# A Mamba-2 scan beside its projections: a product moved from GpSimd to VectorE, and a norm one step later

## The chip, the cores and the metric

The kernel runs on one core of a Trainium2 chip. Its engines work at the same time, each through its own list of instructions in order: TensorE (PE; its weight loads are PEld) multiplies matrices, VectorE (DVE), ScalarE (ACT) and GpSimd (POOL) work element by element, and SyncE (SP) mostly issues DMAs. The metric is the device time of one execution in microseconds (us). Of the kernel before there are three timed runs; one further execution was profiled.

## What is computed

One layer of a hybrid decoder trunk over 1024 tokens of width 1024, in float32: a Mamba-2 (SSD) mixer, a hierarchical mixture of 64 experts, a gated per-layer embedding, and a final norm. The change touches the mixer. Cut to what matters:

```python
def ssd_mixer(u, ...):
    zxbcdt = u @ w_in                       # z, x, B, C, dt
    xbc = silu(causal_depthwise_conv(xbc, conv_w, conv_b))
    y = ssd_chunked_scan(xs, dt, A, Bm, Cm)
    yz = (y + xs * d_skip) * silu(z)
    yg = yz.reshape(L, 4 groups, 512)
    yg = yg * rsqrt(mean(yg * yg, axis=-1) + EPS)   # a norm in each group
    return (yg * gnorm) @ w_out

def ssd_chunked_scan(x, dt, A, Bm, Cm):     # chunks of 128 tokens
    acum = cumsum(dt * A)                   # within a chunk
    decay = exp(where(causal, acum_l - acum_s, -inf))
    w_ls = (C_l . B_s) * decay              # causal B-C product times decay
    y_diag = w_ls @ (x * dt)
    states = B^T @ (x * dt * decay_to_end)
    h = h * chunk_decay + states            # from chunk to chunk
    y_off = (C @ h) * exp(acum)             # reaches the output from earlier chunks
    return y_diag + y_off
```

## The kernel before

The mixer works in eight units: two halves of 512 tokens, in each four groups of eight heads. For a unit, project computes ten tiles of 128 channels (B, C, four of x, four of z), each by 24 matmuls: weights and inputs are split into a high and a low float32r part, and three products (lines 183, 184, 185) are added up over eight steps of depth. split (lines 69 and 70) makes the parts: ScalarE the high half (wh), then VectorE the low one (wl), and the third matmul of a tile (L185) is the first that needs wl. The six tiles of B, C and x then go through a convolution, three multiply-adds on VectorE (L263) and a SiLU.

While a unit is projected, the scan of the unit before it runs beside it, chunk by chunk. The function front(c) prepares a chunk: the cumulative sums come by DMA, spread over all partitions (ac); TensorE transposes x (px, L306) and B and multiplies B with C (pb, L308 and L309) into two buffers of one PSUM pool (tp, two buffers in all); ScalarE takes ec = exp(ac) (L311); VectorE subtracts each token's own sum, eight times 128x128 (L313); ScalarE takes the exponential again (L315). VectorE makes xc = x dt (L317), the masked product cbm (L321), xd (L327) and the weights ac times cbm (L330). GpSimd copies the last column of ec (ed, L325) and multiplies ec with C (L329), except for a sequence's first chunk. back(c) does the matmuls of y (L347, L349) and of the state (L352), the state's update on VectorE (L343, L354), the skip and gate (L360, L362) and the squares (ScalarE, then GpSimd's sums L366 and L367). norm adds the squares over channels on TensorE (L372) and takes the root in thirteen small VectorE instructions (lines 56 to 66); store transposes the roots (L380), scales the four chunks (L383) and writes them to DRAM by SP.

The program is written as a plan of unit steps: after each of the ten projected tiles (steps 0 to 9) the pieces listed for that step are emitted. Fronts stand at steps 0, 1, 3 and 5, backs at 2, 4, 6 and 8, norm at 9, and store at step 0 of the next unit. A scheduler then orders each engine's instructions from this, by its own reckoning of when each is ready; so the order on an engine is not the order written. The last scan runs beside the output product (lines 482 to 484) by a plan of its own.

Of the kernel before, what the change touches and what calls it, by code (L numbers as in the profile page):

```python
# [7 lines left out]
F32 = mybir.dt.float32  # L8
# [4 lines left out]
AF = mybir.ActivationFunctionType  # L13
# [5 lines left out]
DI, NH, HD, NG, NS, Q = 2048, 32, 64, 4, 128, 128  # L19
NCH = T // Q  # L20
# [21 lines left out]
class K:  # L42
# [64 lines left out]
    def ssd(self, left, right):  # L107
        nc, tc, a = self.nc, self.tc, self.a
# [18 lines left out]
        wk = self.pool("wk", 2, **kr)  # L127
# [140 lines left out]
        def project(hf, g):  # L268
            x = X[hf]
            w = load(2 * DI + g * 128, 2 * DI + 512 + g * 128)  # L270
            xT, zT = [], zp.tile([128, 4, HT], F32, name="z")
            bT = conv_tile(hf, w, 0, x, 16 + g)
            yield
            cT = conv_tile(hf, w, 1, x, 20 + g)
            U[hf, g] = bT, cT, xT, zT
            yield
            for j in range(2):
                w = load(DI + g * 512 + j * 256)
                for i in range(2):
                    xT.append(conv_tile(hf, w, i, x, 4 * g + 2 * j + i))  # L280
                    yield
            for j in range(2):
                w = load(g * 512 + j * 256)
                for i in range(2):
                    nc.scalar.activation(zT[:, 2 * j + i], proj(w, i, x), AF.Silu)
                    yield

        def scan(hf, g):

            hs = slice(8 * g, 8 * g + 8)  # L290
# [4 lines left out]
            def front(c):  # L295
                dt_s, acs = SZ[hf]
                bT, cT, xT, zT = U[hf, g]
                cg = hf * HC + c
                cs = slice(c * Q, (c + 1) * Q)
                ac = wk.tile([128, 8, Q], F32, name="ac", bufs=3)  # L300
                nc.sync.dma_start(ac, bass.AP(tensor=acd.tensor, offset=acd[8 * g:8 * g + 1, cg * Q:cg * Q + 1].offset,
                                              ap=[[0, 128], [T, 8], [1, Q]]))
                px = self.ps_tp.tile([128, 8, HD], F32, name="tp")
                pxf = px.rearrange("p h d -> p (h d)")
                for j in range(4):
                    nc.tensor.transpose(pxf[:, j * 128:(j + 1) * 128], xT[j][:, cs], self.ident)  # L306
                pb = self.ps_tp.tile([128, 2, 128], F32, name="tp")
                nc.tensor.transpose(pb[:, 0], bT[:, cs], self.ident)  # L308
                nc.tensor.matmul(pb[:, 1], lhsT=bT[:, cs], rhs=cT[:, cs], start=True, stop=True)  # L309
                ec = wk.tile([128, 8, Q], F32, name="ec")  # L310
                nc.scalar.activation(ec, ac, AF.Exp)  # L311
                for h in range(8):
                    nc.vector.tensor_scalar(ac[:, h], ac[:, h], acs[:, c, 8 * g + h:8 * g + h + 1], 0.0,  # L313
                                            op0=OP.subtract, op1=OP.min)
                nc.scalar.activation(ac, ac, AF.Exp)  # L315
                xc = wk.tile([128, 8, HD], F32, name="xc")
                nc.vector.tensor_mul(xc, px, dt_s[:, c, hs][:, :, None].to_broadcast([128, 8, HD]))  # L317
                bt = wk.tile([128, 128], F32, name="bt")
                nc.scalar.activation(bt, pb[:, 0], AF.Copy)
                cbm = wk.tile([128, 128], F32, name="cbm")  # L320
                nc.vector.tensor_mul(cbm, pb[:, 1], self.tri)  # L321
                ed = wk.tile([128, 8], F32, name="ed")
                xd = None
                if cg < NCH - 1:
                    nc.gpsimd.tensor_copy(ed, ec[:, :, Q - 1])  # L325
                    xd = wk.tile([128, 8, HD], F32, name="xd")
                    nc.vector.tensor_mul(xd, xc, ac[:, :, Q - 1:Q].to_broadcast([128, 8, HD]))  # L327
                if cg:
                    nc.gpsimd.tensor_mul(ec, ec, cT[:, cs][:, None, :].to_broadcast([128, 8, Q]))  # L329
                nc.vector.tensor_mul(ac, ac, cbm[:, None, :].to_broadcast([128, 8, Q]))  # L330
                V[c] = ac, ec, xc, bt, ed, xd

# [44 lines left out]
            def store():  # L377
# [3 lines left out]
                for c in range(HC):  # L381
# [4 lines left out]
                        yzs[c])  # L386

            return front, back, norm, store

        X, SZ, U = {}, {}, {}  # L390
# [4 lines left out]
        prev, before = None, None  # L395
        units = [(hf, g) for hf in range(2) for g in range(NG)]
        for hf, g in units:
            plan = {}

            def at(t, f, *args):  # L400
                plan.setdefault(t, []).append((f, args))

            if g == 0:
                for t in (0, 1, 7, 8):
                    at(t, next, sizes, None)
            if before:
                at(0, before[3])
            if prev:
                front, back, norm, store = prev
                for t, f, c in ((0, front, 0), (1, front, 1), (2, back, 0), (3, front, 2), (4, back, 1),  # L410
                                (5, front, 3), (6, back, 2), (8, back, 3)):
                    at(t, f, c)
                if (hf, g) != units[-1]:
                    at(9, norm)
            if hf == 0 and g == NG - 1:
                xg = x_half(1)
                for t in (4, 5, 6, 7):
                    at(t, next, xg)
            for t, _ in enumerate(project(hf, g)):
                for f, args in plan.get(t, ()):  # L420
                    f(*args)
            before, prev = prev, scan(hf, g)
            if hf == 0 and g == NG - 1:
                for _ in xg:
                    pass
                sizes = step_sizes(1)
        front, back, norm, store = prev
# [1008 lines left out]
```

## Time and profile before

| | |
|---|---|
| median of three runs | 2008.52 us (2005.11 to 2008.72) |
| profiled execution, device time | 2003.53 us |
| its span, first to last instruction | 2001.7 us |
| busy share of the span | PE 94%, DVE 53%, ACT 37%, POOL 14% |
| granted TensorE clock, mean | 0.971 |

The shares are means over stages with different limits. The stages show in the busy time of stretches: the columns are the stretch, its length, the busy us (and instructions) of PE, PEld, DVE, ACT and POOL, the granted clock, the mean share of the DMA engines and GB/s.

```profile
0.00:84.00 84.00, 68.53 (x319) 55.30 (x320) 46.32 (x90) 39.73 (x57) 17.74 (x39) 0.98 0.46 141
...
690.00:760.00 70.00, 61.68 (x331) 47.77 (x330) 56.55 (x103) 30.63 (x43) 12.77 (x14) 0.95 0.64 205
760.00:940.00 180.00, 165.27 (x835) 134.14 (x835) 120.58 (x333) 62.15 (x90) 32.03 (x54) 0.93 0.74 264
940.00:2001.00 1061.00, 1030.48 (x4329) 399.95 (x4325) 358.41 (x710) 237.19 (x396) 48.74 (x44) 0.99 0.94 376
```

Until 84 us the input is normed and the first group is projected without a scan; from there to 690 us projections and scans run side by side; then the last scan beside the output product, the rest of that product with the router, and from some 940 us the experts. In the rows of waits shown further on, the instruction in front waited for the one behind the arrow, with the sum in us, the number of waits and the longest.

### The profile page before, as it was taken

What the parts mean: (1) busy time and instruction counts of PE and PEld (TensorE: products, weight loads), DVE (VectorE), ACT (ScalarE), POOL (GpSimd) and SP (SyncE); (2) the same over time, 40 slices, a digit from 0 to 9 for tenths busy, and PEclk for the clock granted to TensorE, in tenths of its full rate; (3) what the DMA queues carried; (4) which work ended last, traced back from release to release, by engine and by line L of the source; (5) the groups of instructions that cost most, each with busy time, mean ns of one, the idle gap of its engine ahead of it and who ended that gap; (6) DMA issues with size and microseconds to landing.
All of it is one profiled execution on the core that took longest, in us unless ns stands there. A gap on an engine that the chain in (4) does not pass through costs nothing.

```text
span 2001.7 us, 23417 instructions
## 1 busy us (share of the span) xinstructions
PE 1875.6 (94%) x8822; PEld 1071.1 (54%) x8822; DVE 1060.1 (53%) x2148; ACT 740.7 (37%) x1036; POOL 273.1 (14%) x338
## 2 busy tenths in 40 slices
PE   7989987899999899997999999999999999999996
PEld 5867766677777677884343343333433334334334
DVE  5487886679889687657332341524414234233223
ACT  4466655457667543332121121211212222122123
POOL 1122223223232222011000000000000000000004
PEclk9989998899999999997999999999999999999998
DMA  5333432434543469684999999999999999998883
GB/s 173 104 91 93 118 104 63 110 95 114 130 97 89 128 197 345 225 311 163 388 421 421 373 421 400 398 419 375 420 405 395 420 383 410 415 372 323 341 324 114
DMA packets 190056, 534.73 MB, mean 267 GB/s; under 512 B 15855, under 2 KB 128497, under 8 KB 141809
## 3 DMA queue, kind: packets, MB, share of 16 engines
q1 hardware_dynamic: 175632, 510.53, 69.8%
q10 hardware_dynamic: 11008, 12.94, 1.9%
q0 software_dynamic: 3296, 9.70, 1.3%
q8 instruction: 71, 1.16, 0.2%
q14 instruction: 49, 0.39, 0.1%
HBM read 517.27 MB, written 17.69 MB: 267 GB/s over the span
## 4 chain that ended last, share of the span: by engine, by line
PE 71%; DVE 13%; DMA 7%; issue 4%; ACT 2%; POOL 2%; SPq 0%; ACTq 0%; POOLq 0%; DVEq 0%
PE pup L1004 12%; PE pgate L1004 11%; PE py L1004 11%; PE pq L885 6%; DMA ac<-acd 4%; PE mm L185 3%; PE pc L994 3%; PE mm L184 3%; PE mm L183 3%; DVE ac L313 3%; DVE xbc L263 3%; PE mm L483 3%; PE mm L484 3%; PE mm L482 2%; PE pc L838 2%
## 5 line engine op out<-in xcount | busy, mean ns | idle before, releaser
L183 PE MATMUL mm<-xh,wh 128*128 128x512 f32 x640 | 270.5, 423 | 6.0 <-ACT xh L69 5.9
L185 PE MATMUL mm<-xh,wl 128*128 128x512 f32 x640 | 257.4, 402 | 10.8 <-DVE wl L70 10.6
L184 PE MATMUL mm<-xl,wh 128*128 128x512 f32 x640 | 255.6, 399 | 1.5 <-DVE xl L70 1.5
L1004 PE MATMUL pup<-w,XT 128*64 128x512 f32 x1016 | 239.5, 598 | 0.6 <-DMA w<-in_w_up_dram 0.6
L1004 PE MATMUL pgate<-w,XT 128*64 128x512 f32 x1000 | 231.9, 599 | 0.0
L1004 PE MATMUL py<-w,hT 128*64 128x512 f32 (+1 forms) x1024 | 226.9, 585 | 2.1 <-DMA w<-in_w_down_dram 2.1
L70 DVE TENSOR_TENSOR yx<-py,yx 128x512 fp32r<-128x512 f32 (+1 forms) x68 | 44.8, 659 | 234.3 <-ACT yx L69 234.3
L1004 PEld LDWEIGHTS py<-w,hT 128*64 128x64 f32 x1024 | 70.1, 137 | 145.9 <-issue 138.3
L1004 PEld LDWEIGHTS pup<-w,XT 128*64 128x64 f32 x1016 | 72.0, 136 | 141.5 <-issue 131.7
L185 PEld LDWEIGHTS mm<-xh,wl 128*128 128x128 f32 x640 | 123.1, 192 | 43.5 <-DVE wl L70 16.8
L183 PEld LDWEIGHTS mm<-xh,wh 128*128 128x128 f32 x640 | 124.6, 195 | 37.6 <-ACT xh L69 6.1
L184 PEld LDWEIGHTS mm<-xl,wh 128*128 128x128 f32 x640 | 124.1, 194 | 33.3 <-issue 6.0
L1004 PEld LDWEIGHTS pgate<-w,XT 128*64 128x64 f32 x1000 | 68.6, 136 | 134.2 <-issue 129.6
L313 DVE TENSOR_SCALAR ac<-ac,acs 128x128 f32<-128x128 f32 x256 | 105.6, 472 | 42.0 <-ACT ec L311 42.0
L263 DVE SCALAR_TENSOR_TENSOR xbc<-raw,convw,xbc 128x512 f32<-128x512 f32 x144 | 120.6, 838 | 10.8 <-ACT xbc L261 9.9
L885 PE MATMUL pq<-wpg,vx 128*128 128x512 f32 x256 | 123.1, 607 | 0.0
L70 DVE TENSOR_TENSOR wl<-w,wh 128x1024 fp32r<-128x1024 f32 x80 | 98.0, 1227 | 41.4 <-ACT wh L69 41.3
L69 ACT ACTIVATE wh<-w 128x1024 fp32r<-128x1024 f32 x80 | 83.9, 1052 | 66.4 <-PE mm L184 63.9
L483 PE MATMUL mm<-wl,yh 128*128 128x512 f32 x256 | 101.8, 402 | 3.2 <-DVE wl L494 3.2
L482 PE MATMUL mm<-wh,yh 128*128 128x512 f32 x256 | 99.4, 407 | 3.9 <-ACT wh L493 3.9
L484 PE MATMUL mm<-wh,yl 128*128 128x512 f32 x256 | 100.8, 398 | 0.0
L69 ACT ACTIVATE yx<-py 128x512 fp32r<-128x512 f32 (+1 forms) x68 | 38.9, 572 | 159.4 <-PE py L1004 159.4
(381 smaller groups left out, 2855.1 us busy)
## 6 DMA issues: line engine op xcount, KB each, us to landing
w<-in_w_up_dram SPq DMA_DIRECT2D x127, 1024.0 KB, 9.3
w<-in_w_gate_dram SPq DMA_DIRECT2D x125, 1024.0 KB, 8.7
w<-in_w_down_dram SPq DMA_DIRECT2D x120, 1024.0 KB, 9.3
w<-in_w_in_dram SPq DMA_DIRECT2D x32, 1024.0 KB, 5.4
w<-in_w_out_dram SPq DMA_DIRECT2D x48, 512.0 KB, 4.6
ac<-acd SPq DMA_DIRECT2D x32, 512.0 KB, 9.5
w<-in_w_in_dram SPq DMA_DIRECT2D x16, 512.0 KB, 5.1
yn<-yz SPq DMA_DIRECT2D x32, 256.0 KB, 4.3
```

The costliest lines, as they stand in the source:

```text
L69: self.nc.scalar.activation(dst_h, src, AF.Copy)
L70: self.nc.vector.tensor_sub(dst_l, src, r_(dst_h))
L183: nc.tensor.matmul(ps, lhsT=wh[:, k], rhs=x[0][:, k], start=(k == 0), stop=False)
L184: nc.tensor.matmul(ps, lhsT=wh[:, k], rhs=x[1][:, k], start=False, stop=False)
L185: nc.tensor.matmul(ps, lhsT=wl[:, k], rhs=x[0][:, k], start=False, stop=(k == KD - 1))
L263: nc.vector.scalar_tensor_tensor(o, raw[:, j:j + HT], convw[:, m, j:j + 1], o, op0=OP.mult, op1=OP.add)
L313: nc.vector.tensor_scalar(ac[:, h], ac[:, h], acs[:, c, 8 * g + h:8 * g + h + 1], 0.0, op0=OP.subtract, op1=OP.min)
L482: nc.tensor.matmul(po[i][hf], lhsT=yh[:, ts], rhs=wh[:, cs], start=(k == 0), stop=False)
L483: nc.tensor.matmul(po[i][hf], lhsT=yh[:, ts], rhs=wl[:, cs], start=False, stop=False)
L484: nc.tensor.matmul(po[i][hf], lhsT=yl[:, ts], rhs=wh[:, cs], start=False, stop=(k == 15))
L885: nc.tensor.matmul(V["pq"], lhsT=V["vT"][:, k], rhs=wpg[:, k, cs], start=(k == 0), stop=(k == KD - 1))
L1004: nc.tensor.matmul(ps[64 * b:64 * b + 64], lhsT=xt(k0 + k, b), rhs=w[b][:, k, cs], start=(k0 + k == 0), stop=(k0 + k == K - 1))
```

## The change

Three edits in the scan. The product of ec and C, and the copy of ec's last column, run on VectorE in place of GpSimd. xc, bt and the masked product cbm are written ahead of the exponential and the subtractions. norm moves from step 9 to step 0 of the next unit, and store from step 0 to step 2.

```diff
@@ -307,26 +307,27 @@
                 pb = self.ps_tp.tile([128, 2, 128], F32, name="tp")
                 nc.tensor.transpose(pb[:, 0], bT[:, cs], self.ident)
                 nc.tensor.matmul(pb[:, 1], lhsT=bT[:, cs], rhs=cT[:, cs], start=True, stop=True)
+                xc = wk.tile([128, 8, HD], F32, name="xc")
+                nc.vector.tensor_mul(xc, px, dt_s[:, c, hs][:, :, None].to_broadcast([128, 8, HD]))
+                bt = wk.tile([128, 128], F32, name="bt")
+                nc.scalar.activation(bt, pb[:, 0], AF.Copy)
+                cbm = wk.tile([128, 128], F32, name="cbm")
+                nc.vector.tensor_mul(cbm, pb[:, 1], self.tri)
                 ec = wk.tile([128, 8, Q], F32, name="ec")
                 nc.scalar.activation(ec, ac, AF.Exp)
                 for h in range(8):
                     nc.vector.tensor_scalar(ac[:, h], ac[:, h], acs[:, c, 8 * g + h:8 * g + h + 1], 0.0,
                                             op0=OP.subtract, op1=OP.min)
                 nc.scalar.activation(ac, ac, AF.Exp)
-                xc = wk.tile([128, 8, HD], F32, name="xc")
-                nc.vector.tensor_mul(xc, px, dt_s[:, c, hs][:, :, None].to_broadcast([128, 8, HD]))
-                bt = wk.tile([128, 128], F32, name="bt")
-                nc.scalar.activation(bt, pb[:, 0], AF.Copy)
-                cbm = wk.tile([128, 128], F32, name="cbm")
-                nc.vector.tensor_mul(cbm, pb[:, 1], self.tri)
                 ed = wk.tile([128, 8], F32, name="ed")
                 xd = None
                 if cg < NCH - 1:
-                    nc.gpsimd.tensor_copy(ed, ec[:, :, Q - 1])
+                    nc.vector.tensor_copy(ed, ec[:, :, Q - 1])
+                if cg:
+                    nc.vector.tensor_mul(ec, ec, cT[:, cs][:, None, :].to_broadcast([128, 8, Q]))
+                if cg < NCH - 1:
                     xd = wk.tile([128, 8, HD], F32, name="xd")
                     nc.vector.tensor_mul(xd, xc, ac[:, :, Q - 1:Q].to_broadcast([128, 8, HD]))
-                if cg:
-                    nc.gpsimd.tensor_mul(ec, ec, cT[:, cs][:, None, :].to_broadcast([128, 8, Q]))
                 nc.vector.tensor_mul(ac, ac, cbm[:, None, :].to_broadcast([128, 8, Q]))
                 V[c] = ac, ec, xc, bt, ed, xd
 
@@ -404,14 +405,13 @@
                 for t in (0, 1, 7, 8):
                     at(t, next, sizes, None)
             if before:
-                at(0, before[3])
+                at(0, before[2])
+                at(2, before[3])
             if prev:
                 front, back, norm, store = prev
                 for t, f, c in ((0, front, 0), (1, front, 1), (2, back, 0), (3, front, 2), (4, back, 1),
                                 (5, front, 3), (6, back, 2), (8, back, 3)):
                     at(t, f, c)
-                if (hf, g) != units[-1]:
-                    at(9, norm)
             if hf == 0 and g == NG - 1:
                 xg = x_half(1)
                 for t in (4, 5, 6, 7):
```

What the scheduler makes of it shows in the order of instructions on an engine; out<-in are the names of the kernel, with buffer numbers. In the changed kernel the lines are numbered anew: L311 is xc, L315 cbm, L319 the subtractions, L325 the copy ed, L327 the product ec, L330 xd, L331 ac times cbm.

First place: VectorE where the first two fronts begin (ac_746 and xc_767 or xc_756 are the first front's, ac_817 the second's). Before:

```order
L313 TENSOR_SCALAR ac_746<-ac_746,acs_379 128x128 x8
L313 TENSOR_SCALAR ac_817<-ac_817,acs_379 128x128 x2
L317 TENSOR_TENSOR xc_767<-tp_748,dt_s_378 128x512
L313 TENSOR_SCALAR ac_817<-ac_817,acs_379 128x128 x5
L327 TENSOR_TENSOR xd_775<-xc_767,ac_746 128x512
L263 SCALAR_TENSOR_TENSOR xbc_740<-raw_707,convw_102,xbc_740 128x512
L321 TENSOR_TENSOR cbm_771<-tp_753,jp_58 128x128
L263 SCALAR_TENSOR_TENSOR xbc_740<-raw_707,convw_102,xbc_740 128x512
L330 TENSOR_TENSOR ac_746<-ac_746,cbm_771 128x1024
```

and now:

```order
L319 TENSOR_SCALAR ac_746<-ac_746,acs_379 128x128 x8
L325 COPY ed_773<-ec_762 128x8
L319 TENSOR_SCALAR ac_817<-ac_817,acs_379 128x128
L311 TENSOR_TENSOR xc_756<-tp_748,dt_s_378 128x512
L319 TENSOR_SCALAR ac_817<-ac_817,acs_379 128x128 x2
L315 TENSOR_TENSOR cbm_760<-tp_753,jp_58 128x128
L319 TENSOR_SCALAR ac_817<-ac_817,acs_379 128x128 x3
L263 SCALAR_TENSOR_TENSOR xbc_740<-raw_707,convw_102,xbc_740 128x512
L319 TENSOR_SCALAR ac_817<-ac_817,acs_379 128x128
L263 SCALAR_TENSOR_TENSOR xbc_740<-raw_707,convw_102,xbc_740 128x512
L330 TENSOR_TENSOR xd_775<-xc_756,ac_746 128x512
```

cbm, which frees the PSUM buffer tp_753, moved from behind xd and a convolution step to the middle of the second front's subtractions; the copy ed came in.

Second place: TensorE around the store of the first group (tp_1384 before, tp_1529 now; mm are projections). Before:

```order
L184 MATMUL mm_1351<-xl_201,wh_1347 128x512
L185 MATMUL mm_1351<-xh_200,wl_1348 128x512
L380 MATMUL tp_1384<-ident_60,rs_1323 128x128 x4
L306 MATMUL tp_1399<-ident_60,xbc_885 128x128
L306 MATMUL tp_1399<-ident_60,xbc_947 128x128
L306 MATMUL tp_1399<-ident_60,xbc_1021 128x128
```

and now:

```order
L183 MATMUL mm_1496<-xh_200,wh_1492 128x512
L184 MATMUL mm_1496<-xl_201,wh_1492 128x512
L185 MATMUL mm_1496<-xh_200,wl_1493 128x512
L381 MATMUL tp_1529<-ident_60,rs_1367 128x128 x4
L348 MATMUL py_1543<-ac_1384,xc_1394 64x128 x8
L353 MATMUL pst_1552<-xd_1413,bt_1396 128x512
```

The store moved behind the transposes of the next unit's first two fronts, to just ahead of its first back. Between the norm's last matmul and the store there stood one projection, mm_1351; now there are two, mm_1422 and mm_1496. Two of the norm's four matmuls now stand some 100 matmuls ahead of the other two.

Third place: VectorE late in the seventh unit, at the fourth front of the sixth scan (ac_4537) and the split wl_4570 that the next projection needs. Before:

```order
L263 SCALAR_TENSOR_TENSOR xbc_4461<-raw_4429,convw_102,xbc_4461 128x512
L362 TENSOR_TENSOR yz_4489<-yz_4489,z_3480 128x512
L263 SCALAR_TENSOR_TENSOR xbc_4461<-raw_4429,convw_102,xbc_4461 128x512
L313 TENSOR_SCALAR ac_4537<-ac_4537,acs_2919 128x128 x8
L70 TENSOR_TENSOR wl_4570<-w_4567,wh_4569 128x1024
L317 TENSOR_TENSOR xc_4558<-tp_4539,dt_s_2918 128x512
L343 TENSOR_TENSOR st_4599<-st_4467,ed_4421 128x512
```

and now:

```order
L319 TENSOR_SCALAR ac_4537<-ac_4537,acs_2906 128x128
L263 SCALAR_TENSOR_TENSOR xbc_4461<-raw_4429,convw_102,xbc_4461 128x512
L319 TENSOR_SCALAR ac_4537<-ac_4537,acs_2906 128x128
L263 SCALAR_TENSOR_TENSOR xbc_4461<-raw_4429,convw_102,xbc_4461 128x512
L319 TENSOR_SCALAR ac_4537<-ac_4537,acs_2906 128x128 x3
L311 TENSOR_TENSOR xc_4547<-tp_4539,dt_s_2905 128x512
L319 TENSOR_SCALAR ac_4537<-ac_4537,acs_2906 128x128 x3
L327 TENSOR_TENSOR ec_4553<-ec_4553,xbc_3584 128x1024
L70 TENSOR_TENSOR wl_4570<-w_4567,wh_4569 128x1024
```

The subtractions now stand among convolution steps, and xc and the product ec stand ahead of the split.

## The prediction

> **What bounds the kernel now.** I read the page's span and slices, the busy time by stretch, the list of who waited for whom on TensorE, and then single places in the timeline.
>
> ```profile
> span 2001.7 us, 23417 instructions
> ...
> PE   7989987899999899997999999999999999999996
> ...
> PEclk9989998899999999997999999999999999999998
> ```
>
> TensorE is busy in nearly every slice, but the lower digits, and the lower clock digits below them, lie in the first third, where the scan runs. The next view gives, for a stretch, its length, the busy time (and instructions) of PE, PEld, DVE, ACT and POOL, the granted clock, the DMA share and GB/s.
>
> ```profile
> 84.00:690.00 606.00, 549.61 (x3015) 433.95 (x3013) 478.24 (x916) 371.04 (x452) 161.86 (x187) 0.95 0.41 102
> 760.00:2001.00 1241.00, 1195.75 (x5162) 534.09 (x5160) 479.00 (x1042) 299.33 (x485) 80.78 (x98) 0.98 0.91 360
> ```
>
> From 84 to 690 us, the units with a scan beside a projection, TensorE is idle 606 - 549.6 = 56.4 us, and VectorE 127.8 us. So TensorE sets the pace and VectorE now and then holds it up. Behind 760 us stand the experts, whose work the change does not touch; I take what the scan saves to pass through whole. The waits of TensorE in the scan's stretch (total, times, longest):
>
> ```profile
> PE mm L185 <- DVE wl L70: 9.8, 7, 2.5
> PE tp L380 <- DVE rs L66: 7.6, 3, 2.8
> PE tp L308 <- DVE cbm L321: 6.6, 1, 6.6
> PE tp L372 <- POOL sqs L367: 5.9, 3, 2.2
> ```
>
> These four, 29.9 of the 56.4 us, are waits the change can reach: for the low half of a split weight (L70), for a group's norm (L372 waits for the last chunk's sum of squares, L380 for the root), and once for the masked product. They also cost clock. The same columns as above, for stretches right behind such waits:
>
> ```profile
> 108.00:115.00 7.00, 5.65 (x15) 3.87 (x16) 7.00 (x16) 5.58 (x8) 0.29 (x2) 0.50 0.07 10
> 173.00:176.40 3.40, 3.40 (x9) 2.82 (x10) 0.40 (x3) 0.96 (x1) 0.00 (x0) 0.50 0.23 40
> 183.20:186.60 3.40, 3.40 (x12) 2.91 (x11) 2.44 (x4) 3.39 (x5) 0.19 (x1) 0.50 0.41 92
> 254.90:258.30 3.40, 3.40 (x10) 2.66 (x9) 0.00 (x0) 2.13 (x2) 0.00 (x0) 0.50 0.12 19
> 452.90:456.30 3.40, 3.34 (x11) 2.24 (x10) 3.40 (x6) 3.39 (x4) 0.00 (x0) 0.50 0.26 39
> 524.50:528.00 3.50, 3.50 (x10) 2.74 (x9) 2.04 (x8) 3.37 (x4) 0.00 (x0) 0.51 0.26 34
> 572.30:575.70 3.40, 3.40 (x10) 2.62 (x9) 2.72 (x5) 1.69 (x3) 0.00 (x0) 0.50 0.00 0
> 647.40:650.80 3.40, 3.40 (x9) 2.66 (x9) 2.77 (x5) 1.63 (x3) 0.00 (x0) 0.50 0.00 0
> ```
>
> In each the clock is half, so half of PE's busy time there is lost: 2.8 us in the first, 8.5 us in the next five (behind norm waits), 3.4 us in the last two (behind L70 waits).
>
> **The first front.** All sums are against the profiled execution, 2003.5 us, which is 5.0 us under the median of the runs shown.
>
> ```profile
> 107.51 0.28 DVE L321 TENSOR_TENSOR cbm<-tp,jp 128x128 f32<-128x128 f32 x1
> 107.84 0.48 PE L308 MATMUL tp<-ident,xbc 128*128 128x128 f32 x1 [6.58 <-DVE cbm L321]
> ```
>
> The second front's transpose waits 6.6 us for a PSUM buffer that the first front's masked product still has to read. That product stands on VectorE behind the subtractions, xd and a convolution step; in the new order it stands before these. Gain **6.6 + 2.8 = 9.4 us**; what is late next there is the exponential's DMA, which bounds the gain from below at nothing, if xc is held up instead.
>
> **Norm and store.**
>
> ```profile
> 171.67 0.72 POOL L366 TENSOR_TENSOR sq<-sq 128x256 f32<-128x256 f32 x1 [8.45 <-ACT sq L365]
> 172.98 0.59 PE L372 MATMUL tp<-ones,sqs 128*128 128x1 f32 x2 [2.24 <-POOL sqs L367]
> 182.54 0.16 DVE L66 SCALAR_TENSOR_TENSOR rs<-nt,nt 128x4 f32<-128x4 f32 x1
> 182.76 0.72 PE L380 MATMUL tp<-ident,rs 128*128 128x128 f32 x4 [2.23 <-DVE rs L66]
> ```
>
> Here the norm comes one projection after the last chunk, and its root one projection before the store. Moved a step later, the last sum of squares has a whole projection more, and the store, which goes from step 0 to step 2, has two projections for the root instead of one. Gain **7.6 + 5.9 + 8.5 = 22.0 us**, from nothing (if the root is late again) to all. The four stores of a unit also leave SP two steps later, behind the next loads; of the six yz buffers the moved step frees four before the third chunk needs one, so I cost that at nothing. Without that cover a chunk would wait for a store's landing.
>
> **The product on VectorE.**
>
> ```profile
> L329 POOL TENSOR_TENSOR ec<-ec,xbc 128x1024 f32<-128x1024 f32 x28 | 71.9, 2569 | 26.4 <-ACT ec L311 24.5
> L313 DVE TENSOR_SCALAR ac<-ac,acs x256: 270/276/2499, 95.1 to 727.3; 128x128 f32<-128x128 f32 x128
> L313 DVE TENSOR_SCALAR ac<-ac,acs 128x128 f32<-128x128 f32 x256 | 105.6, 472 | 42.0 <-ACT ec L311 42.0
> L330 DVE TENSOR_TENSOR ac<-ac,cbm x32: 1210/1218/3401, 108.4 to 731.8; 128x1024 f32<-128x1024 f32 x32
> L64 DVE TENSOR_TENSOR nt<-nt x30: 147/161/164, 15.4 to 753.0; 128x4 f32<-128x4 f32 x24, 128x3 f32<-128x3 f32 x6
> 564.58 3.02 POOL L329 TENSOR_TENSOR ec<-ec,xbc 128x1024 f32<-128x1024 f32 x1 [4.67 <-ACT ec L311]
> 565.26 4.48 DVE L313 TENSOR_SCALAR ac<-ac,acs 128x128 f32<-128x128 f32 x8
> 569.67 1.21 DVE L70 TENSOR_TENSOR wl<-w,wh 128x1024 fp32r<-128x1024 f32 x1
> 570.93 0.50 PE L185 MATMUL mm<-xh,wl 128*128 128x512 f32 x1 [2.47 <-DVE wl L70]
> ```
>
> Added to VectorE: 28 products of L330's shape and broadcast at 1.218 us, 34.1 us. The 28 copies have no row on VectorE; between L64's 161 ns (its size) and L313's 276 ns (one source, 16 times as wide) I take the first: 4.5 us, at most 7.7. Together 38.6 us. Released: a subtraction takes 276 ns, but up to 2499 ns while GpSimd runs L329, as at 565.26 us, where eight take 4.48 us. Over the group that is 256 x (472 - 276) ns = 50.2 us, and I take that; the ends are nothing (if the blocking only used idle time) and 71.9 us, all of L329. So VectorE's load falls by some 12 us although work comes to it, and it stays at about three quarters busy.
>
> What decides is what stands ahead of a split. The wait at 570.93 us, and with it the other L70 waits, follow a blocked row of subtractions: gain **9.8 + 3.4 = 13.2 us**, none at worst. Against it, in the new order 12 of the 28 products stand within three rows ahead of a split, on which a TensorE product is queued, and all later projections behind it: 12 x 1.218 = **14.6 us of new waits**, between none and 28 x 1.218 = 34.1 us. The new TensorE order also switches between projection and scan 192 times up to the output product, not 174. The start of a scan run costs
>
> ```profile
> PEld py L347 <- issue: 7.4, 21, 0.7
> ```
>
> 7.4 / 21 = 0.35 us, so nine more starts cost **3.2 us**; none if hidden, 6.3 if every switch pays. GpSimd loses 28 products and copies; it keeps the additions of L366, which now wait for nothing of its own.
>
> Sum: 9.4 + 22.0 + 13.2 - 14.6 - 3.2 = 26.8 us less: 2003.5 - 26.8 = 1976.7 us; on the footing of the median, 5.0 us above, **1982 us**.
>
> **Two rules of the Trainium skill.** The Trainium skill, "TensorE: Matmul & The Clock Gate", section "Why this matters for your kernels", says that only PE gaps over about 3 us bring half clock back. By it waits of 2.2 to 2.8 us would cost no clock, and the sum would lose 11.9 us of its gain; here the trace disagrees, since the seven half-clock stretches after the first start right behind such short waits. The Trainium skill, "SBUF — State Buffer", section "Who interferes with whom", says that a VectorE instruction with two SBUF inputs and a GpSimd instruction that reads SBUF exclude each other, whichever starts second waiting the whole time out. That speaks against the move, as the product has two such inputs and L366 stays; by it each product could wait for one, and by L330's row, of the same kind, whose median is its minimum within 8 ns, it hardly does.
>
> **Rivals.** (a) The new waits do not come, because the released time always lies ahead of the split: 14.6 and 3.2 us less, 1976.7 - 17.8 + 5.0 = 1964 us. For it speaks the row of 565.26 us, 2.8 us longer than eight unblocked ones; against it that products now stand right ahead of splits. (b) The norm moves but its wait moves along: its thirteen small VectorE instructions are queued one by one between convolutions and splits, the root is late again, and the 22.0 us do not come: 1998.7 + 5.0 = 2004 us. For it speaks that in the trace those at 173 to 182 us are spread in just this way; against it the second projection of cover. This is also the case in which the change does little of what it says. (c) Slower: VectorE becomes what paces the projections. Place: the splits in each unit; price: all 38.6 us stand ahead of splits and nothing released comes back there, so the L70 gain goes, and each of seven units gets a half-clock window of 1.7 us, 11.9 us: -9.4 - 22.0 + 38.6 + 3.2 + 11.9 = +22.3 us, 2031 us. It decides as soon as less than 22.3 of the 50.2 us comes back ahead of splits. For it: VectorE is busy 79% of the stretch, strictly in order, with 127.8 us of slack that lies where it waits for others. Against: 565.26 us again.
>
> **How the numbers follow.** Forecast 0.47, (a) 0.14, (b) 0.22, (c) 0.17. The range reaches from below (a) to 2008 us, above (b), and leaves (c) and some of (a) out: 1960 to 2008 us. A measurement tells about 0.2%, 4 us, from no change. (b) lies on that bound and is split: faster 0.47 + 0.14 + 0.12 = 0.73, same 0.10, slower 0.17.
>
> **What would show it.** In the profile after: no 6.6 us wait of the second front; L372 and L380 waits near nothing, and the half-clock stretches behind them gone; the subtractions' mean near 276 ns; the product at 1.2 us on VectorE; L70 waits of TensorE no longer than now in sum. If L70 waits grow past 20 us, (c) is under way; if the store's wait for the root is still some 7 us, (b). Wrong in kind would be a gain that comes behind 760 us.

## The result, and the profile after

| | before | after |
|---|---|---|
| median of four runs | 2007.20 us (2005.11 to 2008.72) | 1971.26 us (1970.56 to 1972.58) |
| profiled execution, device time | 2003.53 us | 1971.61 us |
| its span | 2001.7 us | 1969.6 us |
| granted TensorE clock, mean | 0.971 | 0.982 |

The time is 0.9831 of that before, with a 95% interval of 0.9819 to 0.9844: 34 us faster. The page of the changed kernel has TensorE's busy tenths in 40 slices and the granted clock in tenths:

```profile
PE   6989997899999899997999999999999999999996
...
PEclk9999998999999999998999999999999999999998
```

The first third has fewer low digits: one of TensorE's less, and one 8 of the clock where there were three. The next view splits the span where the same work ends: the units with a scan, up to the first matmul of the output product; the last scan beside that product, up to the router's first transpose. The columns are stretch, length, busy us (and instructions) of PE, PEld, DVE, ACT and POOL, granted clock, DMA share, GB/s. The kernel before:

```profile
84.00:686.80 602.80, 546.41 (x3000) 431.63 (x2998) 475.04 (x908) 369.97 (x451) 161.67 (x186) 0.95 0.41 102
686.80:756.30 69.50, 62.85 (x334) 48.64 (x334) 56.05 (x107) 29.35 (x41) 12.96 (x15) 0.95 0.61 194
```

The kernel after:

```profile
84.00:659.50 575.50, 536.47 (x3004) 425.25 (x3002) 457.32 (x958) 372.93 (x452) 87.08 (x133) 0.97 0.42 107
659.50:722.90 63.40, 60.98 (x328) 47.27 (x329) 54.08 (x112) 32.34 (x44) 8.96 (x12) 0.97 0.68 216
```

The units take 27.3 us less and the last scan 6.1 us less. From there to the end both kernels take the same: 2001.7 - 756.3 = 1245.4 us and 1969.6 - 722.9 = 1246.7 us. In the units TensorE's idle time falls from 602.8 - 546.4 = 56.4 to 39.0 us, by 17.4 us; its busy time falls by 9.9 us for the same matmuls, since they get the full clock more often. VectorE is busy 17.7 us less although it does more. TensorE's waits in the units of the kernel after (sum, times, longest):

```profile
PE mm L185 <- DVE wl L70: 10.4, 7, 3.7
...
PE py L348 <- DVE yz L361: 2.6, 1, 2.6
```

No wait of the norm's sums (L373) or of the root's transposes (L381) is left, and the 6.6 us for cbm are 0.3 us. The splits' waits (L70) stay as they were, 10.4 for 9.8 us. VectorE's groups of the kernel after, from 84 to 760 us (busy us, mean ns of one, idle before):

```profile
L263 DVE SCALAR_TENSOR_TENSOR xbc<-raw,convw,xbc 128x512 f32<-128x512 f32 x126 | 96.6, 767 | 2.6 <-ACT xbc L261 2.0
...
L319 DVE TENSOR_SCALAR ac<-ac,acs 128x128 f32<-128x128 f32 x256 | 66.1, 319 | 31.6 <-ACT ec L317 31.6
...
L327 DVE TENSOR_TENSOR ec<-ec,xbc 128x1024 f32<-128x1024 f32 x28 | 36.4, 1300 | 0.3
```

and the convolution before, which the prediction did not look at:

```profile
L263 DVE SCALAR_TENSOR_TENSOR xbc<-raw,convw,xbc 128x512 f32<-128x512 f32 x126 | 107.1, 851 | 9.8 <-ACT xbc L261 9.2
```

The subtractions took 105.6 us and take 66.1, the convolution 107.1 and 96.6: 50.0 us come back. The product costs 36.4 us, and 28 copies some 6 us. (A group's durations add up neighbours that overlap: eight subtractions of 276 ns take 1.65 us where nothing holds them up. So these sums don't come out at exactly the 17.7 us.) The profile fits the forecast in the main, though the subtractions' mean is 319 ns and not near 276, and it would have been easy to stop here. Which edit earned the 34 us, it does not say.

### The profile page after: what moved, and what is told of

It is laid out like the page before. It is cut to its first block, busy times and chain, and to the rows that moved or that the text cites. A ratio compares the mean times of both kernels' runs of the same rounds, so it can differ in the third digit from the quotient of the medians.

```text
span 1969.6 us, 23423 instructions
## 1 busy us (share of the span) xinstructions
PE 1862.9 (95%) x8822; PEld 1063.3 (54%) x8822; DVE 1037.4 (53%) x2204; ACT 746.5 (38%) x1040; POOL 195.0 (10%) x282
## 4 chain that ended last, share of the span: by engine, by line
PE 79%; DVE 8%; DMA 7%; ACT 2%; issue 2%; POOL 1%; SPq 0%; POOLq 0%; ACTq 0%; DVEq 0%
PE pgate L1004 11%; PE pup L1004 11%; PE py L1004 10%; PE mm L185 6%; PE mm L183 6%; PE pq L885 6%; PE mm L184 6%; PE pc L994 3%; DMA w<-in_w_up_dram 3%; PE mm L483 2%; PE mm L482 2%; PE mm L484 2%; DMA ac<-acd 2%; PE pc L838 2%; PE pc L1067 2%
## 5 line engine op out<-in xcount | busy, mean ns | idle before, releaser
L183 PE MATMUL mm<-xh,wh 128*128 128x512 f32 x640 | 264.9, 414 | 5.7 <-ACT xh L69 4.6
L70 DVE TENSOR_TENSOR yx<-py,yx 128x512 fp32r<-128x512 f32 (+1 forms) x68 | 44.8, 660 | 232.6 <-ACT yx L69 232.6
L70 DVE TENSOR_TENSOR wl<-w,wh 128x1024 fp32r<-128x1024 f32 x80 | 97.6, 1222 | 50.3 <-ACT wh L69 50.3
L263 DVE SCALAR_TENSOR_TENSOR xbc<-raw,convw,xbc 128x512 f32<-128x512 f32 x144 | 110.0, 764 | 3.6 <-ACT xbc L261 2.6
L1035 ACT ACTIVATE hT<-pt 128x512 f32<-128x512 f32 x31 | 18.4, 594 | 211.4 <-PE pt L1033 211.4
```

What stands on the lines that cost most here:

```text
L70: self.nc.vector.tensor_sub(dst_l, src, r_(dst_h))
L183: nc.tensor.matmul(ps, lhsT=wh[:, k], rhs=x[0][:, k], start=(k == 0), stop=False)
L263: nc.vector.scalar_tensor_tensor(o, raw[:, j:j + HT], convw[:, m, j:j + 1], o, op0=OP.mult, op1=OP.add)
```

## Experiments

Each ratio is to the kernel before, run on the same chip; "in the units" is the length of the stretch from 84 us to the output product, from the run's profile (602.8 us before, 575.5 us after).

### The edits one by one

The norm edit alone:

```diff
             if before:
-                at(0, before[3])
+                at(0, before[2])
+                at(2, before[3])
...
-                if (hf, g) != units[-1]:
-                    at(9, norm)
```

> Only the norm and the store move a step later; product and copy stay on GpSimd, cbm stays behind the subtractions. Theory A (each edit has its own waits): TensorE's waits for L372 and L380, 13.5 us, and the five half-clock stretches behind them, 8.5 us, go, and nothing else: 22 us less, ratio to before 0.989. The 6.6 us wait for cbm and the L70 waits stay. Theory B (the gain is the scheduler's new order, which only the three edits together give): within 8 us of before, ratio 0.996 to 1.004.

Measured: 2017.98 us, ratio 1.0073 (1.0050 to 1.0095). It is slower by 13.5 us, where the term of the sum said 22 us faster. TensorE's waits between 84 and 690 us of this kernel, which has the line numbers of before, one less behind the edit:

```profile
PE tp L308 <- DVE nt L56: 16.0, 3, 6.9
PE mm L185 <- DVE wl L70: 13.1, 10, 2.2
```

The waits of L372 and L380, 13.5 us before, are gone from this stretch; one of 5.0 us for the sums (L372) is left behind 690 us. In their place the next unit's fronts wait 16.0 us for L56, the norm's first VectorE instruction, and the splits' waits grow by 3.3 us. The timeline at the first such place (start, duration, engine, and in brackets the wait ahead of it):

```profile
176.71 0.95 PE L372 MATMUL tp<-ones,sqs 128*128 128x1 f32 x8
...
180.04 3.76 DVE L313 TENSOR_SCALAR ac<-ac,acs 128x128 f32<-128x128 f32 x8 [8.25 <-ACT ec L311]
...
180.34 2.40 POOL L329 TENSOR_TENSOR ec<-ec,xbc 128x1024 f32<-128x1024 f32 x1
...
184.85 0.15 DVE L56 TENSOR_SCALAR nt<-tp 128x4 f32<-128x4 f32 x1
...
185.06 0.48 PE L308 MATMUL tp<-ident,xbc 128*128 128x128 f32 x1 [6.91 <-DVE nt L56]
```

The sums were there at 177.7 us. L56 is queued behind eight subtractions, which wait for ec; these then take 3.76 us beside GpSimd's product, and a split follows. All that time the sums hold one of the two tp buffers.

The product edit alone, product and copy on VectorE and nothing else:

```diff
-                    nc.gpsimd.tensor_copy(ed, ec[:, :, Q - 1])
+                    nc.vector.tensor_copy(ed, ec[:, :, Q - 1])
...
-                    nc.gpsimd.tensor_mul(ec, ec, cT[:, cs][:, None, :].to_broadcast([128, 8, Q]))
+                    nc.vector.tensor_mul(ec, ec, cT[:, cs][:, None, :].to_broadcast([128, 8, Q]))
```

> Only the product and the copy run on VectorE; norm and cbm as before. Theory A: blocking by GpSimd goes (subtractions' mean from 472 to under 330 ns), the load on VectorE falls by some 12 us; the L70 waits do not change in sum, but the last scan, where VectorE and TensorE are about level, gets shorter by some 6 us, and the norm's root comes earlier: 6 to 16 us less, ratio 0.992 to 0.997. Theory C (work moved to the busier engine costs): slower by 5 us or more, and the change wins only by its other two edits.

Measured: 1974.85 us, ratio 0.9861 (0.9840 to 0.9881), 30 us faster. The units of this kernel, in the columns of the stretches above:

```profile
84.00:658.40 574.40, 536.92 (x3008) 425.88 (x3006) 459.94 (x956) 370.36 (x451) 94.08 (x133) 0.96 0.42 107
```

and two of its waits:

```profile
PE tp L381 <- DVE rs L66: 4.9, 2, 3.4
PE tp L373 <- POOL sqs L368: 3.6, 1, 3.6
```

This edit alone makes the units as short as the whole change does, and takes 5.0 of the 13.5 us off the norm's own waits (L380 and L372 in the kernel before), although it doesn't touch the norm. It does not shorten the last scan, which takes 69.6 us here. The splits' waits (L70) are 2.4 us in this kernel, for 9.8 before. And no matmul of the kernel before waited for the product itself: L349, which reads it, has no wait in TensorE's list. So by this list the product does not cost by its own time on the way to TensorE.

The early order alone (xc, bt and cbm ahead of the exponential):

```diff
+                xc = wk.tile([128, 8, HD], F32, name="xc")
...
+                nc.vector.tensor_mul(cbm, pb[:, 1], self.tri)
                 ec = wk.tile([128, 8, Q], F32, name="ec")
```

> Only xc, bt and cbm are written ahead of the subtractions. Theory A: the second front's 6.6 us wait and part of its half clock go, 4 to 9 us less, ratio 0.995 to 0.998; all other waits stay. Theory B: no difference, since the scheduler places by readiness and not by the order written.

Measured: 1997.83 us, ratio 0.9968 (0.9957 to 0.9979), 7 us faster. The wait for cbm, which this edit was to end, is still 4.0 us.

### The edits two by two

The whole change without the norm edit, which stands at step 9 and step 0 again:

> The change without its norm edit: product on VectorE and cbm early, norm at step 9 and store at step 0 as before. Theory A: what is missing from the change's 36 us is the norm's 22 us: 14 us less than before, ratio 0.993, with waits for L372 and L380 of about 13 us. Theory B: near the change or near before, with no such split.

Measured: 1970.29 us, ratio 0.9839 (0.9821 to 0.9857), which can't be told from the whole change's 0.9831. Within the change the norm edit is worth nothing that these runs can tell, and what was expected here, that the gain shrinks by most of the norm's term, did not come. The splits' wait in this kernel's units shows where its gain goes, in part:

```profile
PE mm L185 <- DVE wl L70: 5.3, 6, 1.4
```

The norm's own waits are 8.9 us here: L373 waits 3.9 us for L368 and 4.3 us for L311, and L381 0.7 us. The norm edit ends them, and the splits' waits grow from 5.3 to 10.4 us. Units and last scan together take 642.7 us without the norm edit and 638.9 us with it, but the times of the two kernels don't show these 3.8 us.

The whole change without the product edit (product and copy back on GpSimd):

> The change without its product edit: norm later and cbm early, product and copy on GpSimd. Theory A', formed on the runs so far (the product edit is the gain; the norm edit loses while GpSimd blocks VectorE, because its PSUM buffer is then released late): the sum of the single edits, +14 and -6 us against before: 5 to 12 us slower, with waits for L56 in TensorE's list. Rival B (the three edits help each other through the order): faster than before by 10 us or more.

Measured: 2012.99 us, ratio 1.0049 (1.0033 to 1.0064). Without the product edit the change is slower than the kernel before. With the early order in place the norm edit costs 1.0049 - 0.9968 = 0.8% while GpSimd has the product, as it does alone (0.7%), and nothing once VectorE has it (0.9831 for 0.9839).

### Why the product's engine matters

Two kernels answer this together. Both are the kernel after with 19 further products of the same shape, in the scans of the last five units, written into a buffer that nothing reads any more; only the engine differs:

```diff
                 if cg:
+                    if hf or g == NG - 1:
+                        junk = g_bc.rearrange("p (h q) -> p h q", h=8)
+                        nc.gpsimd.tensor_mul(junk, *[cT[:, cs][:, None, :].to_broadcast([128, 8, Q])] * 2)
                     nc.vector.tensor_mul(ec, ec, cT[:, cs][:, None, :].to_broadcast([128, 8, Q]))
```

On GpSimd:

> The changed kernel with one more product on GpSimd in each front from the fifth unit on (19 of them): 128x1024, two SBUF inputs, written to a buffer that nothing reads any more. Nothing waits for its result. If GpSimd's product holds VectorE up while it runs, the blocking comes back for 19 of 28 fronts: 52.8 x 19/28 = 36 us more on VectorE, subtractions' mean above 380 ns, and some two thirds of the product edit's 28 us lost: 10 to 20 us slower than the changed kernel (1971 us). If it was the product's own time on the way to TensorE (2.4 us on GpSimd, 1.2 on VectorE), no difference.

On VectorE:

> The changed kernel with the same 19 products of no use on VectorE instead: 19 x 1.22 = 23 us more work on VectorE. If VectorE's load as such comes through to TensorE, 15 to 23 us slower than the changed kernel. If its slack takes it up (some 125 us idle in the units), under 8 us. If work for work it costs less than the same product on GpSimd does in the run beside it, the blocking is worse than the load.

Measured: 1994.55 us, ratio 0.9957 (0.9939 to 0.9975), with them on GpSimd; 1975.59 us, ratio 0.9855 (0.9832 to 0.9878), on VectorE. So on GpSimd, which is idle most of the time, they cost 23 us, and on VectorE, the busier engine, some 4 us, which lies within the noise of these runs. The units show the same, first with GpSimd:

```profile
84.00:684.80 600.80, 545.23 (x3012) 431.92 (x3009) 477.62 (x959) 374.28 (x454) 127.17 (x152) 0.96 0.39 102
```

then with VectorE:

```profile
84.00:664.90 580.90, 540.47 (x2998) 427.89 (x2996) 478.17 (x976) 370.95 (x451) 96.13 (x133) 0.96 0.40 106
```

VectorE is busy just as long in both, 477.6 and 478.2 us, and 457.3 us without the 19 products: in the first it spends the 20.3 us on instructions that stand still, as their number is the same but for one (959 and 958), in the second on work. How it stands still shows in the timeline of the first:

```profile
462.61 8.13 POOL L329 TENSOR_TENSOR g_bc<-xbc 128x1024 f32<-128x1024 f32 x4
...
467.27 1.72 DVE L263 SCALAR_TENSOR_TENSOR xbc<-raw,convw,xbc 128x512 f32<-128x512 f32 x1 [0.65 <-ACT xbc L261]
468.92 2.38 DVE L366 TENSOR_TENSOR yz<-yz,z 128x512 f32<-128x512 f32 x1
...
471.88 1.21 DVE L70 TENSOR_TENSOR wl<-w,wh 128x1024 fp32r<-128x1024 f32 x1
...
473.14 0.80 PE L185 MATMUL mm<-xh,wl 128*128 128x512 f32 x1 [3.73 <-DVE wl L70]
```

While GpSimd works, a convolution step takes 1.72 for 0.75 us and the gate 2.38 for 0.68 us. Behind them in the queue stands a split, and TensorE waits 3.73 us for it; at the same place it waits 1.07 us in the kernel after and in the one with the products on VectorE. TensorE itself waits for nothing of GpSimd in the units; the cost comes by way of VectorE, in two of TensorE's waits:

```profile
PE mm L185 <- DVE wl L70: 19.6, 9, 3.7
PE py L351 <- DVE yz L364: 9.6, 2, 9.3
```

In the kernel after they are 10.4 and 2.6 us. The second one is only in part a matter of standing still. GpSimd also computes a part of dt for the second half (L217 and L218, in turns), and two of the added products stand in its queue among these:

```profile
378.58 2.44 POOL L329 TENSOR_TENSOR g_bc<-xbc 128x1024 f32<-128x1024 f32 x1
...
389.72 0.29 DVE L219 TENSOR_TENSOR de<-de,ds 128x128 f32<-128x128 f32 x1 [4.95 <-POOL de L218]
...
390.88 0.70 PE L351 MATMUL py<-ac,xc 128*64 128x128 f32 x4 [9.32 <-DVE yz L364]
```

The other one takes 1.89 us, at 381.81. From 378.16 to 389.69 GpSimd needs 11.5 us for what takes it 7.2 us in the kernel after. VectorE waits for that result, the gate's first step (L364) stands behind it in VectorE's queue, and TensorE waits for the gate. So up to 7.0 us of the wait come at least in part from a result of GpSimd that is late, and 9.2 us from splits, of which the first timeline shows one. The product edit has nothing of the first kind: L219 waits 3.9 us for L218 in the kernel before and 4.2 us in the kernel after.

One thing was not as I had expected: the added products are ready early, so they hold up the convolution (L263's mean is 841 ns up to 760 us, 767 without them: 126 x 74 ns = 9.3 of the 20.3 us) and a few others, not the subtractions, whose mean stays at 320 ns. The units grow by 25.3 us: TensorE idles 16.5 us more, and is busy 8.8 us more with the same matmuls, at a lower clock. That 20 us of work on VectorE cost 5.4 us there and 20 us of standing still 25.3 us shows that the load alone doesn't set the cost. What else makes the difference no run separates: the place ahead of splits, as in the first timeline with four products in a row, and the late result of the second one both have a part.

Next, the kernel after without the product:

> The kernel after without the product of ec and C (left out, so the part of y from earlier chunks is not scaled by C; the matmul reads ec as it is). It asks what the 28 products on VectorE cost TensorE. Theory S (slack): the product costs TensorE next to nothing because VectorE waits enough anyway; 19 useless ones more on VectorE cost 4 us, so 28 less gain at most 6: some 1965 to 1971 us, ratio 0.980 to 0.984. Rival (new waits as predicted, 12 of 28 products ahead of a split): 14.6 us less, near 1957 us, ratio 0.976.

Its total says nothing: it ran 14026 us with 35960 matmuls for 8822, presumably because with other values the experts get other tokens. The stages ahead of them can be read:

```profile
84.00:657.10 573.10, 537.05 (x2999) 427.39 (x2998) 426.76 (x936) 372.64 (x450) 86.71 (x133) 0.96 0.41 107
657.10:723.90 66.80, 60.66 (x333) 47.89 (x333) 51.13 (x108) 29.71 (x44) 8.98 (x12) 0.95 0.70 203
```

VectorE is busy 30.6 us less in the units, but they end only 2.4 us earlier, and the router starts at 723.9 us, 1.0 us later than with the product. On VectorE the product costs TensorE next to nothing.

### Why the norm edit loses by itself

To see whether the held tp buffer is the cause, the norm edit alone was run again with the norm's sums in a buffer of the projections' pool, at the places that it moves:

```diff
-            def norm():
-                pm = self.ps_tp.tile([128, HC], F32, name="tp")
+            def norm(mm=False):
+                pm = self.ps_mm.tile([128, 512], F32, name="mm")[:, :HC] if mm else self.ps_tp.tile([128, HC], F32, name="tp")
```

> The norm edit alone, as in e1_norm, but with the norm's sums in one of the four PSUM buffers of the projections (mm) instead of one of the two that the fronts use (tp). If the norm edit lost because its sums hold one of the two tp buffers until VectorE reads them (16 us of waits of L308 for L56), those waits go and it comes out at 5 to 20 us faster than before. If it lost for another reason (the order of the rest), it stays 10 us or more slower.

Measured: 2017.01 us, ratio 1.0071 (1.0049 to 1.0092), no better than 1.0073. The theory of the buffer falls: freeing the fronts' buffer does not bring the loss back. The waits of L308 for L56 did go, but TensorE now waits at the same places for ScalarE's half of a split:

```profile
457.05 1.06 ACT L311 ACTIVATE ec<-ac 128x1024 f32<-128x1024 f32 x1 [5.50 <-DMA ac<-acd]
...
458.14 3.77 DVE L313 TENSOR_SCALAR ac<-ac,acs 128x128 f32<-128x128 f32 x8 [8.65 <-ACT ec L311]
...
464.25 1.04 ACT L69 ACTIVATE wh<-w 128x1024 fp32r<-128x1024 f32 x1
...
465.34 0.80 PE L183 MATMUL mm<-xh,wh 128*128 128x512 f32 x1 [5.03 <-ACT wh L69]
```

ec waits for its DMA, the subtractions for ec, the second exponential for the subtractions, and wh is queued behind that. And with only the store moved, the norm staying at step 9:

```diff
-                at(0, before[3])
+                at(2, before[3])
```

> The kernel before with only the store moved from step 0 to step 2; the norm stays at step 9. It splits the norm edit, which alone was 14 us slower. Theory P (the norm at step 0 stands between the next unit's first fronts and holds them up): without that move the 16 us of waits of L308 for L56 do not come, the root has three projections, and the 7.6 us of L380 for L66 go: 3 to 10 us faster than before, ratio 0.995 to 0.9985. Rival Q (whatever is moved there, VectorE's lateness comes out elsewhere, in the splits): no gain or a loss, ratio 1.000 to 1.007.

Measured: 2011.28 us, ratio 1.0040 (1.0025 to 1.0055): slower, as rival Q has it. Two of its waits:

```profile
PE mm L185 <- DVE wl L70: 15.9, 10, 2.4
PE tp L372 <- POOL sqs L367: 14.5, 5, 4.9
```

The 7.6 us of L380 for L66 are gone, and the splits have 6.1 us more and the sums of squares 8.6 us more. Three kernels thus took a wait of the norm away by moving it, and each time as much or more came out in another place. Why it comes out as a loss of 7 to 14 us and not level stays open: the order on VectorE and ScalarE changes in many places at once, and no run here separates them. What is shown is that the loss goes when GpSimd's product goes.

### More of the same

GpSimd still has the sums of squares. They go to VectorE as well:

```diff
-                nc.gpsimd.tensor_add(sq[:, 0:2], sq[:, 0:2], sq[:, 2:4])
-                nc.gpsimd.tensor_add(sqs[:, c], sq[:, 0], sq[:, 1])
+                nc.vector.tensor_add(sq[:, 0:2], sq[:, 0:2], sq[:, 2:4])
+                nc.vector.tensor_add(sqs[:, c], sq[:, 0], sq[:, 1])
```

> The kernel after with GpSimd's sums of squares (two additions a chunk, 32 chunks) on VectorE as well, so that GpSimd has next to no large work beside the scan. Theory B (blocking by GpSimd is what costs): the subtractions' mean falls from 319 ns to near 275 ns and the product's from 1300 to near 1220, 14 us of VectorE time back, against some 32 x (0.36 + 0.2) = 18 us of additions; load the same, but no long blocked rows: 0 to 6 us faster, 1965 to 1971 us. Rival: VectorE is now the tighter engine and the additions stand ahead of splits: 5 to 15 us slower.

Measured: 1966.00 us, ratio 0.9802 (0.9781 to 0.9822). The row of its subtractions by line (least, median and longest ns, first and last start):

```profile
L319 DVE TENSOR_SCALAR ac<-ac,acs x256: 271/279/289, 95.0 to 689.0; 128x128 f32<-128x128 f32 x128
```

and its units:

```profile
84.00:652.80 568.80, 533.23 (x3004) 422.64 (x3002) 456.91 (x1011) 358.98 (x443) 52.12 (x77) 0.98 0.41 108
```

No subtraction is held up any more: the longest takes 289 ns, for 846 ns in the kernel after and 2499 ns before. VectorE took over 64 additions and is busy no longer, 456.9 for 457.3 us. The same without the norm edit:

> The kernel after with GpSimd's sums of squares on VectorE, as in the run before this, but with norm and store where the kernel before has them. With the three runs that are known it makes a square: sums on GpSimd or on VectorE (0.9831 and 0.9802 with the norm edit), norm edit or not (0.9831 and 0.9839 with the sums on GpSimd). Theory B (work of GpSimd beside the scan costs, the place of the norm does not): as with the norm edit, ratio 0.978 to 0.982, 1961 to 1969 us. Rival 1: the norm edit begins to pay once GpSimd is out of the way, so without it 8 us or more slower, ratio 0.984 or above. Rival 2: the 5 us of the sums were chance, ratio near 0.9835 as well.

Measured: 1966.71 us, ratio 0.9816 (0.9802 to 0.9829). That is theory B's range: the two kernels with the sums on VectorE are at 0.9802 and 0.9816, the two with them on GpSimd at 0.9831 and 0.9839. The gain of some 5 us has the same sign in both pairs, but the intervals touch, so it is likely rather than settled. Both are faster than the kernel before, and at the median 5 us below the kernel after.

## Why the prediction came out

The forecast was 1982 us and the time is 1971. That it came so near is luck: one term was 22 us too high and another some 35 us too low. Rival (a), at 1964 us, is nearer to the time, and it had one of the reasons: the new waits on VectorE do not come.

- **Norm and store, 22.0 us.** This is the first step that failed: I took the waits of L372 and L380 for waits that the norm's place causes, so that two projections of cover would end them. They do end, as the prediction asked the profile to show, yet the term is worth nothing that can be told from noise: 0.9831 with the edit, 0.9839 without, and 1.0073 alone. Rival (b) was right that the wait moves along, but not on where to: it had the root late again at the store, and no such wait is left (L381). Lateness of VectorE that was paid at the norm is paid elsewhere when the norm is moved.
- **The product: 13.2 - 14.6 - 3.2, a net of -4.6 us.** This step failed the other way. It measures 30 us alone, and the change without it is 44 us slower (1.0049 for 0.9831). The 13.2 us for the splits do not show as such in the whole change, where these waits are 10.4 us for 9.8; they are 2.4 us with the product edit alone, and the norm edit brings them back. The 14.6 us of new waits do not come: without the product the units end 2.4 us earlier, and 19 more on VectorE cost 4 us. Rival (a) was right that they don't come. And what is released also pays at waits that I had booked under other edits: at the norm (5.0 us) and at cbm (2.6 us are left of 6.6 with the product edit alone). The prediction counted which instruction TensorE waited for, where it should have asked what made that instruction late. That the nine further starts of scan runs cost 3.2 us was not tried by itself; the row that the price was read from grows by 1.2 us in the units, from 6.7 to 7.9 us.
- **VectorE's load.** 50.2 us released were counted from the subtractions alone. They gave 39.5 us, because GpSimd's sums still hold them up (mean 319, not 276 ns); the convolution gave the other 10.5 us. The product's cost, 34.1 us, is 36.4 us. The balance in the units, some 12 us less, is 17.7 us less.
- **The first front, 9.4 us.** The wait of 6.58 us does end, but the order of cbm earns little of it. The stretch from 95 to 120 us, in the columns of the stretches above, for the kernel before, the product edit alone, the early order alone and the kernel after:

```profile
95.00:120.00 25.00, 16.63 (x73) 12.07 (x71) 18.91 (x40) 14.49 (x20) 6.45 (x10) 0.80 0.40 110
...
95.00:120.00 25.00, 20.11 (x89) 14.79 (x88) 18.37 (x40) 14.43 (x19) 2.43 (x5) 0.86 0.46 124
...
95.00:120.00 25.00, 15.49 (x55) 11.23 (x54) 16.96 (x35) 13.95 (x18) 5.85 (x9) 0.73 0.28 69
...
95.00:120.00 25.00, 20.06 (x92) 14.69 (x91) 19.72 (x44) 16.99 (x22) 1.76 (x6) 0.86 0.35 78
```

  The product edit alone gets TensorE through 89 matmuls where the kernel before does 73 and the whole change 92. The early order alone does 55: it leaves 3.96 us of the wait, and 1.36, 2.64 and 0.84 us of other waits follow. By the matmuls done, its 7 us come later, most of them between 455 and 543 us, where TensorE does 501 for 467; what makes them no run separates. With both edits, what is late next is the first chunk's weights ac, as the timeline of the kernel after shows, and with it, for the last point, a later split:

```profile
101.86 0.33 PE L308 MATMUL tp<-ident,xbc 128*128 128x128 f32 x1 [0.34 <-DVE cbm L315]
...
106.36 1.11 PE L348 MATMUL py<-ac,xc 128*64 128x128 f32 x6 [3.48 <-DVE ac L331]
...
272.83 0.50 PE L185 MATMUL mm<-xh,wl 128*128 128x512 f32 x1 [2.16 <-DVE wl L70]
```

  The 6.58 us of L308 are 0.34 us, and L348 waits 3.48 us a little later, where the prediction had named the exponential's DMA.
- **Rival (c)**, VectorE as the bound, needed all added work ahead of splits and none released there. 19 products more on top of the change still leave the ratio at 0.9855, so VectorE's slack takes them.
- **Two rules weighed.** The hold-up was weighed only against the product in its new place, where it cost little (a mean of 1300 over a median of 1219 ns). The Trainium skill, "SBUF — State Buffer", section "Who interferes with whom", says that the ports which the two engines share are an exclusive lock: one engine has them for a whole instruction, and the other is blocked. The weight of this rule was on the other side, as it speaks for taking the product off GpSimd, and that is where the time was. The run with 19 products on GpSimd agrees with it. The Trainium skill, "TensorE: Matmul & The Clock Gate", section "Why this matters for your kernels", asks for no idle gaps of TensorE over about 3 us, as one idle window brings half clock back. Shorter gaps cost clock in the kernel after as well, as they did before, where the shortest such wait is one of 1.44 us ahead of the stretch at 524.5 us. In the kernel after this stretch at half clock starts 1.5 us behind the split's wait of 2.16 us:

```profile
274.30:277.70 3.40, 3.40 (x9) 2.63 (x9) 3.40 (x9) 0.63 (x1) 0.13 (x1) 0.51 0.13 15
```

Behind the last scan nothing was gained, as forecast: 1245.4 us before and 1246.7 us after.

## What to carry to other kernels

Work on an engine that is busy 14% of the time can still cost 30 of 2005 us, if its long instructions hold up another engine whose queue feeds TensorE: look for a short instruction whose longest time is many times its least, and at what ran beside it. A wait names the instruction that came last, not the cause; if several waits of one engine's late work stand in the list, moving one of them moves the lateness, and an edit that makes the engine earlier pays at all of them. Before booking a gain to each part of a change, ask whether one part takes away the waits that another is meant to hide.

## What was not expected of the hardware

What GpSimd holds up depends on where VectorE reads. In the kernel with 19 products on GpSimd, these are the gate, with two sources in SBUF, and the norm's scaling, whose second source is in PSUM (least, median, longest ns):

```profile
L366 DVE TENSOR_TENSOR yz<-yz,z x32: 678/684/2375, 120.4 to 735.4; 128x512 f32<-128x512 f32 x32
...
L387 DVE TENSOR_TENSOR yz<-yz,tp x32: 673/680/687, 189.6 to 749.5; 128x512 f32<-128x512 f32 x32
```

By the starts and ends in the trace, 17 of the 32 scalings lie beside an arithmetic instruction of GpSimd, and none is longer for it; of the 32 gates one does, and it is the one of 2375 ns. The Trainium skill, "SBUF — State Buffer", section "Who interferes with whom", says so: a VectorE instruction with at most one input in SBUF does not contend with GpSimd, unless it runs in a faster mode that takes both ports. The subtractions have one tensor source and were held up most in sum (a mean of 472 ns for 276, a single one up to 2499), which fits that exception, though no run here tells the mode.
